# An FFN with all 22 column pairs in seven half-size products, two of the seven taken ahead for twelve pairs

## The chip, the cores and the metric

The kernel runs on one core of one Trainium2 chip. TensorE (PE in the profile) multiplies, VectorE (DVE) and ScalarE (ACT) prepare its operands and read its results, SyncE (SP) issues the loads. The metric is the device time of one execution in microseconds; the median of three runs is shown.

## The reference

One layer of a streaming-encoder block on 512 tokens of 1024 features, all in float32:

```python
def swiglu(x, w_gate, w_up, w_down):
    return (jax.nn.silu(x @ w_gate) * (x @ w_up)) @ w_down

h = h + 0.5 * rms_norm(swiglu(rms_norm(h, g1), gate1, up1, down1), g2)   # FFN1
h = h + rms_norm(hybrid_mixer(rms_norm(h, g3), ...), g4)                 # attention and convolution
h = h + 0.5 * rms_norm(swiglu(rms_norm(h, g5), gate2, up2, down2), g6)   # FFN2
```

Gate and up weights are 1024 x 2816, down weights 2816 x 1024. The change touches the first half of the two FFNs: silu(x @ w_gate) * (x @ w_up).

## The kernel before, in words

Every float32 operand is split into a high part (a cast to fp32r, on ACT) and a low part (the operand less its high part, on DVE); `split` issues the two. A product is then three matmuls per 128 x 128 weight tile (`mm3`: high x high, high x low, low x high). So each weight block of 128 x 1024 costs a load of 512 KB into one of three `raw` buffers, a cast on ACT (`whi<-raw`) and a subtraction on DVE (`wlo<-raw,whi`); the two parts lie in a ring of six.

The 2816 hidden features are 22 pairs; pair j is one block of gate weights and one of up weights, 128 features each. Before the change three pairs (`CLASSIC = 3`) are multiplied plainly: 2 blocks x 8 tiles x 3 matmuls over all 512 tokens. `hidden` then takes silu of the gate and multiplies it by up into the buffer `hid`. The other 19 pairs go through `seven_products`, which splits tokens and features in halves and makes the four quarter results of gate and up from seven products instead of eight: 7 x 4 tiles x 3 matmuls of 256 tokens, 84 in all. For this it needs sums of tokens (s1 to s4, `token_sums`, once per FFN: DVE sums, each split on ACT and DVE) and sums of weights for every pair: `t13` (up low half less gate low half, up high less up low) and `t24`. Split operands of a pair are `b` (the gate block itself), `t13`, `t24` and `b22` (the up block's second half).

`periods` runs one period per pair. In the period of pair j, TensorE takes the first three products of j (`b` x a11, `t13` x s1, `t24` x s2), the third products of the pair before, p (`t24` x a22, `b22` x s4), and the second products of j (`b` x a12, `t13` x s3). Meanwhile DVE and ACT prepare the next pair, n, and read the sums of j and p from PSUM. PE, DVE and ACT run in the order in which the code is written (`in_order`), each its own queue. At the start of an FFN the token quarters arrive late (`turn` transposes normed rows and splits them), so the plain pairs run first, on tokens 0 to 255 and then on the rest; the token sums and the first pair's operands (`before`, a generator stepped by `next`) are made beside them. After the 22 pairs comes the product with the down weights (`row_product`, L214), then the mixer, then FFN2 in the same way.

Of the kernel before, what the change touches and what calls it, by code (L numbers as in the profile page):

```python
# [14 lines left out]
P = 128  # L15
S = 512
# [28 lines left out]
CLASSIC = 3  # L45
# [7 lines left out]
def kernel(  # L53
# [41 lines left out]
    blocks = [w[i] for w in (w1, wm, w2) for i in range(w.shape[0])]  # L95
# [75 lines left out]
    def turn(t, xn, u):  # L171

        ts = slice(t * P, (t + 1) * P)
        pss = two_banks()
        for k in range(KD):
            nc.tensor.transpose(pss[k // 4][:, (k % 4) * P:(k % 4 + 1) * P], xn[:, k * P:(k + 1) * P], ident)  # L176
        for b, ps in enumerate(pss):
            ks = slice(4 * b, 4 * b + 4)
            split(u[0][:, ks, ts], u[1][:, ks, ts], ps.rearrange("p (k c) -> p k c", c=P))
# [112 lines left out]
    def token_sums(u, hid, gu):  # L292


        def scratch(i):
            return hid[:, 6 + 2 * i:8 + 2 * i, :].rearrange("p a (b c) -> p (a b) c", c=HALF)

        whole = {q: scratch(4 + i) for i, q in enumerate(((0, 0), (0, 1), (1, 0), (1, 1)))}
        s1, s2, s3, s4 = [scratch(i) for i in range(4)]
        parts = [[gu.tile([P, 4, HALF], F32R, name=f"s{i}{p}") for p in "hl"] for i in (1, 2, 4)]  # L300
        third = [gpool.tile([P, 4, HALF], F32R, name="gain") for _ in range(2)]

        def join(kb, tb):
            q = quadrant(u, kb, tb)
            nc.vector.tensor_tensor(out=whole[kb, tb], in0=q[0].bitcast(F32), in1=q[1].bitcast(F32), op=ALU.add)

        def early():
            join(0, 0)
            join(1, 0)


        def first():
            join(0, 1)
            join(1, 1)
            nc.vector.tensor_tensor(out=s1, in0=whole[0, 1], in1=whole[1, 1], op=ALU.add)
            nc.vector.tensor_tensor(out=s2, in0=s1, in1=whole[0, 0], op=ALU.subtract)
            split(*parts[0], s1)
            split(*parts[1], s2)

        def second():  # L320
            nc.vector.tensor_tensor(out=s4, in0=whole[1, 0], in1=s2, op=ALU.subtract)
            nc.vector.tensor_tensor(out=s3, in0=whole[0, 0], in1=whole[0, 1], op=ALU.subtract)
            split(*parts[2], s4)
            split(*third, s3)

        return parts[0], parts[1], third, parts[2], (early, first, second)

    def seven_products(u, sums, hid, gu, j0, acts):
# [4 lines left out]
        s1, s2, s3, s4, _ = sums  # L333
# [4 lines left out]
        def load(j):  # L338
            if j < NF:
                fetch(2)  # L340
                raw[j] = coming.pop(0), coming.pop(0)
# [20 lines left out]
        def parts(j, n):  # L362
            high(j, n)
            low(j, n)
# [9 lines left out]
        def product(ps, j, n, half, a, start=False):  # L374
            w = ops[j][n][0]
            for k in range(4):
                c0 = half * 512 + k * P

                mm3(ps[:, 0:HALF], part(w, ALLP, slice(c0, c0 + P)), part(a, ALLP, k), start and k == 0, k == 3,
                    skip_group_check=not start)  # L380

        def first_products(j):
            g[j] = [bank() for _ in range(3)]
            product(g[j][0], j, "b", 0, a11, start=True)
            product(g[j][2], j, "t13", 0, s1, start=True)
            product(g[j][1], j, "t24", 0, s2, start=True)

        def second_products(j):
            p7 = g[j][1], j, "t13", 1, s3
            p2 = g[j][0], j, "b", 1, a12  # L390

            for p in (p7, p2) if j == NF - 1 else (p2, p7):
                product(*p)

        def third_products(j):
            product(g[j][1], j, "t24", 1, a22)
            product(g[j][2], j, "b22", 0, s4)

        def silu(out, src):
            nc.scalar.activation(out=out, in_=src, func=AF.Silu)  # L400

        def before():

            load(j0)
            sums13(j0)
            parts(j0, "b")
            parts(j0, "t13")
            sums24(j0)
            yield
            parts(j0, "t24")  # L410
            yield
            parts(j0, "b22")
            load(j0 + 1)
# [8 lines left out]
        def first_sum(j):  # L422
            xs[j] = wide()
            nc.scalar.copy(out=xs[j][:, q[0]], in_=g[j][0][:, q[0]])

        def second_sum(j):
            add(xs[j][:, q[1]], g[j][1][:, q[0]], xs[j][:, q[0]])

        def periods():
            for j in range(j0, NF + 1):  # L430
                p, n = j - 1, j + 1
                old, now, new = p >= j0, j < NF, n < NF
                if old:
                    x, (g1, g2, g3) = xs[p], g[p]
                    y = ys[p] = wide()
                    add(x[:, q[2]], g2[:, q[0]], x[:, q[0]])
                    add(y[:, q[3]], g3[:, q[0]], x[:, q[2]])
                    silu(y[:, q[0]], g1[:, q[0]])
                if now:
                    first_products(j)  # L440
                if new:
                    sums13(n)
                    parts(n, "b")
                elif now:
                    prefetch(1)
                if now:
                    first_sum(j)

                if j == j0:
                    second_sum(j)  # L450
                    sums24(n)
                    parts(n, "t13")
                elif new:
                    parts(n, "t13")
                    second_sum(j)
                    sums24(n)
                elif now:
                    prefetch(2)
                    second_sum(j)
                if old:  # L460
                    third_products(p)
                    add(x[:, q[3]], g2[:, q[0]], x[:, q[0]])
# [10 lines left out]
                load(j + 2)  # L473
# [3 lines left out]
        return before(), periods  # L477

    def ffn(u, steps, post, late, pre=None, turned=None, between=None, weave=False):


        with tc.tile_pool(name="ffn_h", bufs=1) as hp:
            hid = hp.tile([P, NF, S], F32, name="hid")

            def hidden(j, ps):
                sh = wide()
                later["silu"] = nc.scalar.activation(out=sh[:, 0:S], in_=ps[0], func=AF.Silu)
                nc.vector.tensor_tensor(out=hid[:, j, :], in0=sh[:, 0:S], in1=ps[1], op=ALU.mult)

            with tc.tile_pool(name="ffn_gu", bufs=1) as gu:  # L490
                acts = []
                sums = token_sums(u, hid, gu)
                early, first, second = sums[-1]
                before, periods = seven_products(u, sums, hid, gu, CLASSIC, acts)
                ws = []
                head = len(steps)
                pss = [two_banks() for _ in range(head // 2)]
                with in_order():
                    for lo in (0, HALF):
                        for i in range(head):  # L500
                            if lo == 0:
                                for step in steps[i]:
                                    (step or early)()
                                ws.append(weight(0))
                            if lo == 0 and weave and i < 2:
                                for j, n in ((), ((0, 0), (0, 1), (1, 0), (0, 2), (1, 1), (1, 2)))[i]:
                                    one_part(ws[j], u, pss[0][j], 0, HALF, n)
                                continue
                            columns(ws[i], u, pss[i // 2][i % 2], lo, lo + HALF, by_part=lo == 0)
                        if lo == 0:  # L510
                            prefetch(2 * CLASSIC - head)
                            first()
                    hidden(0, pss[0])
                    next(before)
                    hidden(1, pss[1])
# [3 lines left out]
                with in_order():  # L519
                    next(before)  # L520
                    second()
                    for j in range(2, CLASSIC):
                        if j >= len(pss):
                            pss.append(two_banks())
                            for ps in pss[j]:
                                columns(weight(0), u, ps)
                        hidden(j, pss[j])
                    next(before, None)
# [13 lines left out]
    xns = {}  # L542

# [17 lines left out]
    def turned0(t):  # L561
        turn(t, xns[t][0], u1)
# [65 lines left out]
    with tc.tile_pool(name="mix", bufs=1) as mix:  # L628
# [240 lines left out]
        with tc.tile_pool(name="mixb", bufs=1) as mb:  # L869
# [60 lines left out]
            def turned2(t):  # L930
                if not u2:
                    u2.append(new_u())
                turn(t, xns[t], u2[0])
# [99 lines left out]
```

## Time and profile before

| | |
|---|---|
| median of three runs | 1038.58 us (1038.31 to 1040.38) |
| the profiled execution | 1038.58 us, of which the span is 1036.5 us |
| TensorE busy in the span | 1028.9 us (99%) |
| VectorE busy | 773.0 us (75%) |
| ScalarE busy | 476.0 us (46%) |
| loads of 512 KB, issue to landing | 3.6 us |

The profile is of the run that is also the median; some 2 us lie around the span. In the timeline views a row begins with its start in us from the span's start and its length; in square brackets stands the idle time of the engine ahead of it and who ended it.

### The profile page before, as it was taken

Reading aid. Unit: us, or ns where it says so; the run is one execution under the profiler, and the core shown is the slowest. Engines: PE = TensorE matmul, PEld = TensorE weight load, DVE = VectorE, ACT = ScalarE, POOL = GpSimd, SP = SyncE. Lnnn points to the kernel's source line nnn. Section 1 sums busy time; section 2 is a strip of 40 time slices with the busy share of each in tenths; the row PEclk is TensorE's granted clock in tenths of the full one; section 3 lists DMA queues with packets and bytes.
Section 4 is the critical chain, followed back from the end, with each engine's and each line's share of the span. In section 5 each row is a group of like instructions: output and inputs, shape, how many; then the busy total and the mean of one; then the engine's idle time right before and its main releaser. Section 6 shows DMA issues by size and latency. Waiting matters only on the chain.

```text
span 1036.5 us, 16089 instructions
## 1 busy us (share of the span) xinstructions
PE 1028.9 (99%) x6527; PEld 936.1 (90%) x6527; DVE 773.0 (75%) x1188; ACT 476.0 (46%) x785; POOL 20.3 (2%) x42
## 2 busy tenths in 40 slices
PE   9999999999999999999999999999999999999997
PEld 8999999998888898888888888899999999988886
DVE  7999989896332659999869776489989898963314
ACT  6444444444321532677874444354444444442311
POOL 1000000000000100000000100010000000000000
PEclk9999999999999999999999999999999999999999
DMA  6233333336333033433222145131433333353202
GB/s 244 67 103 101 113 98 117 102 114 197 97 102 102 26 119 99 128 95 99 87 77 62 41 131 172 44 102 42 116 98 113 102 102 103 126 181 91 92 21 82
DMA packets 30044, 106.40 MB, mean 103 GB/s; under 512 B 3457, under 2 KB 4105, under 8 KB 29970
## 3 DMA queue, kind: packets, MB, share of 16 engines
q1 hardware_dynamic: 27648, 100.41, 31.0%
q10 hardware_dynamic: 2322, 4.97, 1.5%
q8 instruction: 51, 0.84, 0.3%
q14 instruction: 23, 0.19, 0.1%
HBM read 103.25 MB, written 2.12 MB: 102 GB/s over the span
## 4 chain that ended last, share of the span: by engine, by line
PE 97%; DVE 2%; ACT 1%; issue 0%; DVEq 0%; POOLq 0%; POOL 0%; ACTq 0%
PE ps L214 27%; PE ps L131 20%; PE ps L133 20%; PE ps L132 20%; PE ps L196 5%; PE ps L176 1%; PE ps L832 1%; PE ps L815 1%; DVE acc L643 1%; PE ps L805 0%; PE ps L804 0%; PE ps L275 0%; DVE ptl L93 0%; PE ps L569 0%; DVE wlo L93 0%
## 5 line engine op out<-in xcount | busy, mean ns | idle before, releaser
L131 PE MATMUL ps<-uh,whi 128*128 128x256 f32 (+1 forms) x808 | 254.7, 315 | 0.0
L133 PE MATMUL ps<-uh,wlo 128*128 128x256 f32 (+1 forms) x808 | 252.7, 313 | 0.0
L132 PE MATMUL ps<-ul,whi 128*128 128x256 f32 (+1 forms) x808 | 252.6, 313 | 0.0
L93 DVE TENSOR_TENSOR wlo<-raw,whi 128x1024 fp32r<-128x1024 f32 x108 | 131.5, 1221 | 132.5 <-ACT whi L92 130.7
L92 ACT CAST whi<-raw 128x1024 fp32r<-128x1024 f32 x108 | 112.8, 1051 | 164.6 <-PE ps L214 126.9
L214 PE MATMUL ps<-whi,act 128*128 128x512 f32 x640 | 172.7, 389 | 0.0
L133 PEld LDWEIGHTS ps<-uh,wlo 128*128 128x128 f32 x808 | 154.2, 191 | 9.0
L132 PEld LDWEIGHTS ps<-ul,whi 128*128 128x128 f32 x808 | 154.3, 191 | 8.0
L131 PEld LDWEIGHTS ps<-uh,whi 128*128 128x128 f32 x808 | 154.2, 191 | 8.0
L368 ACT CAST whi<-t 128x1024 fp32r<-128x1024 f32 x76 | 79.8, 1051 | 174.6 <-DVE t L344 165.6
L214 PEld LDWEIGHTS ps<-whi,act 128*128 128x128 f32 x640 | 120.0, 188 | 24.8
L372 DVE TENSOR_TENSOR wlo<-t,whi 128x1024 fp32r<-128x1024 f32 x76 | 93.1, 1226 | 29.1 <-ACT whi L368 29.0
L214 PE MATMUL ps<-wlo,act 128*128 128x512 f32 x320 | 99.3, 389 | 0.0
L643 DVE SCALAR_TENSOR_TENSOR acc<-c,ch,acc 128x512 f32<-128x512 f32 x120 | 86.2, 746 | 1.5
L344 DVE TENSOR_TENSOR xn<-ps,xn 128x256 f32<-128x256 f32 x190 | 79.5, 419 | 5.0 <-PE ps L133 3.6
L214 PEld LDWEIGHTS ps<-wlo,act 128*128 128x128 f32 x320 | 60.1, 188 | 12.5
L344 DVE TENSOR_TENSOR t<-raw,t 128x512 f32<-128x512 f32 x76 | 52.2, 687 | 1.3
L344 DVE TENSOR_TENSOR t<-raw 128x512 f32<-128x512 f32 x76 | 48.8, 684 | 0.0
L372 DVE TENSOR_TENSOR wlo<-raw,whi 128x1024 fp32r<-128x1024 f32 x38 | 46.3, 1219 | 0.0
L131 PE MATMUL ps<-gain,whi 128*128 128x256 f32 x152 | 43.2, 284 | 0.0
L131 PE MATMUL ps<-s1h,whi 128*128 128x256 f32 x152 | 43.0, 283 | 0.0
L132 PE MATMUL ps<-s1l,whi 128*128 128x256 f32 x152 | 43.0, 283 | 0.0
(203 smaller groups left out, 1903.3 us busy)
## 6 DMA issues: line engine op xcount, KB each, us to landing
raw<-in_w SPq DMA_DIRECT2D x132, 512.0 KB, 3.6
raw<-in_wm SPq DMA_DIRECT2D x52, 512.0 KB, 3.6
gain<-in_gains ACTq DMA_DIRECT2D x5, 512.0 KB, 4.0
h<-in_x SPq DMA_DIRECT2D x4, 512.0 KB, 7.6
out<-h SPq DMA_DIRECT2D x3, 512.0 KB, 2.6
bias<-tab_d ACTq DMA_DIRECT2D x8, 128.0 KB, 3.1
bias<-tab_d ACTq DMA_DIRECT2D x8, 112.0 KB, 2.9
out<-xn SPq DMA_DIRECT2D x1, 256.0 KB
```

Source lines behind the costliest of these rows:

```text
L92: nc.scalar.copy(out=hi, in_=src)
L93: nc.vector.tensor_tensor(out=lo, in0=src, in1=hi.bitcast(F32), op=ALU.subtract)
L131: nc.tensor.matmul(ps, a[0], b[0], start=start, stop=False, **kw)
L132: nc.tensor.matmul(ps, a[0], b[1], start=False, stop=False, **kw)
L133: nc.tensor.matmul(ps, a[1], b[0], start=False, stop=stop, **kw)
L176: nc.tensor.transpose(pss[k // 4][:, (k % 4) * P:(k % 4 + 1) * P], xn[:, k * P:(k + 1) * P], ident)
L196: nc.tensor.matmul(ps[:, lo:hi], w[wi][:, k * P:(k + 1) * P], u[ui][:, k, lo:hi], start=i == 0 and k == 0, stop=i == 2 and k == KD - 1)
L214: nc.tensor.matmul(acc[n], a[ai], w[bi][:, n * 512:(n + 1) * 512], start=start and i == 0, stop=stop and i == 2)
L344: nc.vector.tensor_tensor(out=out, in0=a, in1=b, op=op)
L368: nc.scalar.copy(out=h_, in_=src)
L372: nc.vector.tensor_tensor(out=l_, in0=src, in1=h_.bitcast(F32), op=ALU.subtract)
L643: nc.vector.scalar_tensor_tensor(acc[:, j, :], cs[j][:, w:w + S], wc, acc[:, j, :], op0=ALU.mult, op1=ALU.add)
```

## The change

All 22 pairs go through `seven_products`; `CLASSIC` and `hidden` are gone. For the pairs 0 to 11 (`EARLY = 12`) the two products of `b` are taken ahead: `early_products` multiplies the gate block by tokens 0 to 255, keeps the first product (`hid[:, j, 0:HALF]`) and silu of the sum of both (`hid[:, j, HALF:]`). These twelve stand where the plain pairs stood. When such a pair comes up in `periods`, it has no `b`: five products, 60 matmuls; the other ten pairs keep seven. `ORDER` mixes the two kinds. The gate blocks of the twelve are loaded twice, once for `early_products` and once as part of their pair.

The token sums and the first pair's operands are made in eight steps (`first` and `before`, four each) between the early products; the last two sums (`second`) follow in the first period. `turn` writes the unsplit tokens (`whole`) by a second ACT copy from PSUM where before DVE added the two parts.

```diff
-CLASSIC = 3
+EARLY = 12
+ORDER = [12, 0, 13, 1, 14, 2, 15, 3, 4, 16, 5, 17, 6, 7, 18, 8, 19, 9, 10, 20, 11, 21]
@@ turn @@
             split(u[0][:, ks, ts], u[1][:, ks, ts], src)
+            if whole:
+                nc.scalar.copy(out=whole[b, 1][:, :, t % 2 * P:(t % 2 + 1) * P], in_=src)
@@ token_sums: first and second @@
+            nc.vector.tensor_tensor(out=s12, in0=whole[0, 1], in1=whole[1, 1], op=ALU.add)
+            high(s1, s12)
+            yield
+            low(s1, s12)
+            yield
+            nc.vector.tensor_tensor(out=s12, in0=s12, in1=whole[0, 0], op=ALU.subtract)
+            high(s2, s12)
+            yield
+            low(s2, s12)
+            yield
...
@@ seven_products @@
-            ops[j] = {"b": (pair_tiles(), gate), "t13": (pair_tiles(), t13)}
+            ops[j] = {"t13": (pair_tiles(), t13)}
+            if j >= EARLY:
+                ops[j]["b"] = pair_tiles(), gate
...
+        def early_products(j, w):
+            ps = bank()
+            product(ps, w, 0, a11, start=True)
+            nc.scalar.copy(out=hid[:, j, 0:HALF], in_=ps[:, 0:HALF])
+            product(ps, w, 1, a12)
+            later["silu"] = silu(hid[:, j, HALF:], ps[:, 0:HALF])
...
         def periods():
-            for j in range(j0, NF + 1):
+            for i in range(NF + 1):
+                p, j, n = [ORDER[x] if 0 <= x < NF else None for x in (i - 1, i, i + 1)]
...
-                    silu(y[:, q[0]], g1[:, q[0]])
+                    if g1:
+                        silu(y[:, q[0]], g1[:, q[0]])
+                    else:
+                        nc.scalar.copy(out=y[:, q[0]], in_=hid[:, p, HALF:])
                 if now:
                     first_products(j)
+                if i == 0:
+                    second()
                 if new:
                     sums13(n)
                     parts(n, "b")
...
@@ ffn @@
+                        if j >= head:
+                            prefetch(min(2, EARLY - j))
+                            for _ in range(8 * (j + 1 - head) // (EARLY - head) - 8 * (j - head) // (EARLY - head)):
+                                next(todo.pop(0))
...
+                        early_products(j, weight(0))
```

Two places in the order of the instructions. The first is VectorE's queue in a steady period of FFN1. Before, with the next pair's `t13` as t_729 and `t24` as t_743:

```order
L344 TENSOR_TENSOR xn<-ps,xn 128x256 x2
L344 TENSOR_TENSOR t_729<-raw 128x512 x2
L372 TENSOR_TENSOR wlo<-raw,whi 128x1024
L372 TENSOR_TENSOR wlo<-t_729,whi 128x1024
L344 TENSOR_TENSOR xn<-ps,xn 128x256
L344 TENSOR_TENSOR t_743<-raw,t_729 128x512
L344 TENSOR_TENSOR t_743<-raw,t_743 128x512
L344 TENSOR_TENSOR xn<-ps,xn 128x256
L372 TENSOR_TENSOR wlo<-t_743,whi 128x1024
L344 TENSOR_TENSOR xn<-ps,xn 128x256
L470 TENSOR_TENSOR hid<-xn 128x512
L372 TENSOR_TENSOR b22l<-raw,b22h 128x512
```

VectorE's queue in the change, in the period in which pair 1, one of the twelve, is the next (`t13` is t_934, `t24` t_944):

```order
L366 TENSOR_TENSOR xn<-ps,hid 128x256
L366 TENSOR_TENSOR xn<-ps,xn 128x256
L366 TENSOR_TENSOR t_934<-raw 128x512 x2
L397 TENSOR_TENSOR wlo<-t_934,whi 128x1024
L366 TENSOR_TENSOR xn<-ps,xn 128x256
L366 TENSOR_TENSOR t_944<-raw,t_934 128x512
L366 TENSOR_TENSOR t_944<-raw,t_944 128x512
L366 TENSOR_TENSOR xn<-ps,hid 128x256
L397 TENSOR_TENSOR wlo<-t_944,whi 128x1024
L366 TENSOR_TENSOR xn<-ps,xn 128x256
L528 TENSOR_TENSOR hid<-xn 128x512
L397 TENSOR_TENSOR b22l<-raw,b22h 128x512
```

The row `wlo<-raw,whi`, the low part of `b`, is gone from between the sums of `t13` and the low part of `t13`; all else stands where it stood. For a next pair that is not one of the twelve the queue is as before.

The second is ScalarE's queue in FFN1 in the change, between the early products of the gates 5 and 9 (a `CAST whi<-raw` is the high part of a coming gate block, an `ACTIVATE hid<-ps` the silu of a finished early product, which TensorE must have ended):

```order
L452 ACTIVATE hid<-ps 128x256
L94 CAST whi<-raw 128x1024
L316 CAST s2h<-hid 128x1024
L652 DMA tab_d<-xn 8x640
L430 COPY hid<-ps 128x256
L452 ACTIVATE hid<-ps 128x256
L94 CAST whi<-raw 128x1024
L430 COPY hid<-ps 128x256
L452 ACTIVATE hid<-ps 128x256
L94 CAST whi<-raw 128x1024
L393 CAST whi<-t_553 128x1024
```

These silus are of the gates 5, 6 and 7, and the casts behind them those of the gates 7, 8 and 9: a gate's cast stands behind the silu of the gate two before it. Before, no cast of a weight block of the plain pairs stood behind a silu.

## Rows read from the trace of the kernel before

**Rows 1.** The page: the span, and each engine's busy time, share and instructions.

```profile
span 1036.5 us, 16089 instructions
PE 1028.9 (99%) x6527; PEld 936.1 (90%) x6527; DVE 773.0 (75%) x1188; ACT 476.0 (46%) x785; POOL 20.3 (2%) x42
```

**Rows 2.** Stretches of FFN1 (start and periods): length, busy per engine, granted clock, DMA.

```profile
10.00:58.50 48.50, 48.50 (x356) 46.39 (x355) 45.95 (x57) 24.92 (x35) 2.03 (x4) 0.98 0.37 119
58.50:230.00 171.50, 171.50 (x1431) 171.50 (x1431) 154.36 (x237) 77.70 (x120) 0.00 (x0) 1.00 0.34 104
```

**Rows 3.** Timeline of TensorE: plain pair, one product in two periods, start of down products.

```profile
46.36 0.39 PE L131 MATMUL ps<-uh,whi 128*128 128x512 f32 x1
46.59 0.39 PE L132 MATMUL ps<-ul,whi 128*128 128x512 f32 x1
...
103.19 0.28 PE L131 MATMUL ps<-gain,whi 128*128 128x256 f32 x1
...
113.27 0.28 PE L131 MATMUL ps<-gain,whi 128*128 128x256 f32 x1
...
238.55 0.63 PE L214 MATMUL ps<-whi 128*128 128x512 f32 x2
...
910.50 0.63 PE L214 MATMUL ps<-whi 128*128 128x512 f32 x2
```

**Rows 4.** Timeline of VectorE in one period of FFN1.

```profile
106.89 0.88 DVE L344 TENSOR_TENSOR xn<-ps,xn 128x256 f32<-128x256 f32 x2
107.68 1.28 DVE L344 TENSOR_TENSOR t<-raw 128x512 f32<-128x512 f32 x2
108.88 1.22 DVE L372 TENSOR_TENSOR wlo<-raw,whi 128x1024 fp32r<-128x1024 f32 x1
110.08 1.23 DVE L372 TENSOR_TENSOR wlo<-t,whi 128x1024 fp32r<-128x1024 f32 x1
...
111.56 1.41 DVE L344 TENSOR_TENSOR t<-raw,t 128x512 f32<-128x512 f32 x2
...
114.14 1.23 DVE L372 TENSOR_TENSOR wlo<-t,whi 128x1024 fp32r<-128x1024 f32 x1 [0.83 <-ACT whi L368]
...
117.01 0.88 DVE L344 TENSOR_TENSOR xn<-ps,xn 128x256 f32<-128x256 f32 x2
```

**Rows 5.** Timeline of ScalarE in the same period.

```profile
103.89 0.41 ACT L400 ACTIVATE xn<-xn 128x256 f32<-128x256 f32 x1
...
106.91 0.38 ACT L424 COPY xn<-ps 128x256 f32<-128x256 f32 x1
109.00 1.05 ACT L368 CAST whi<-t 128x1024 fp32r<-128x1024 f32 x1 [1.72 <-DVE t L344]
```

**Rows 6.** Timeline of VectorE: first and last of FFN1's 17 steady `hid` products.

```profile
65.17 0.69 DVE L470 TENSOR_TENSOR hid<-xn 128x512 f32<-128x512 f32 x1
...
227.22 0.69 DVE L470 TENSOR_TENSOR hid<-xn 128x512 f32<-128x512 f32 x1
```

**Rows 7.** Timeline of VectorE: last token split, first period's low parts, FFN1 and FFN2.

```profile
22.13 1.29 DVE L93 TENSOR_TENSOR ul<-ps,uh 128x512 fp32r<-128x512 f32 x2
...
53.29 2.42 DVE L372 TENSOR_TENSOR wlo<-t,whi 128x1024 fp32r<-128x1024 f32 x2
...
698.69 1.29 DVE L93 TENSOR_TENSOR ul<-ps,uh 128x512 fp32r<-128x512 f32 x2 [0.35 <-ACT uh L92]
...
725.56 2.42 DVE L372 TENSOR_TENSOR wlo<-t,whi 128x1024 fp32r<-128x1024 f32 x2
```

**Rows 8.** The load queue's waits in FFN1's periods (total, times, longest); landing times.

```profile
SPq L103 <- DVE t L344: 96.0, 17, 5.7
...
DMA to landing us min/median/max: 3.4/3.5/4.4
```

**Rows 9.** Stretches of 1 us at the start (columns as in rows 2).

```profile
9.00:10.00 1.00, 1.00 (x6) 1.00 (x6) 1.00 (x2) 0.69 (x3) 0.00 (x0) 0.50 1.01 414
...
13.00:14.00 1.00, 1.00 (x11) 1.00 (x9) 1.00 (x1) 1.00 (x3) 0.52 (x1) 1.00 0.53 213
```

More of the change, by code (lines that the diff above doesn't have):

```diff
@@ L292, in token_sums @@
     def token_sums(u, hid, gu):
[L295 to L305, printed above, removed]
+        whole = {}
@@ new lines, in token_sums, with high, low @@
+        for i, x in enumerate(((0, 0), (0, 1), (1, 0), (1, 1))):
+            at = hid[:, 14 + 2 * i:16 + 2 * i, :]
+            whole[x] = at.rearrange("p a (b c) -> p (a b) c", c=HALF)
+        s12 = whole[1, 1]
+        s1, s2, s4 = [[gu.tile([P, 4, HALF], F32R, name=f"s{i}{p}") for p in "hl"] for i in (1, 2, 4)]
+        s3 = [gpool.tile([P, 4, HALF], F32R, name="gain") for _ in range(2)]
+        def high(s, src):
+            nc.scalar.copy(out=s[0], in_=src)
+        def low(s, src):
+            nc.vector.tensor_tensor(out=s[1], in0=src, in1=s[0].bitcast(F32), op=ALU.subtract)
@@ L332, in seven_products @@
+        return s1, s2, s3, s4, whole, (early, first(), second)
+    def seven_products(u, sums, hid, gu, acts):
         a11, a12, a22 = quadrant(u, 0, 0), quadrant(u, 1, 0), quadrant(u, 1, 1)
-        s1, s2, s3, s4, _ = sums
+        s1, s2, s3, s4, _, (_, _, second) = sums
         raw, ops, g, xs, ys = {}, {}, {}, {}, {}
@@ L382, in first_products @@
         def first_products(j):
[L383 to L386, printed above, removed]
-        def second_products(j):
[L389 to L393, printed above, removed]
-        def third_products(j):
-            product(g[j][1], j, "t24", 1, a22)
-            product(g[j][2], j, "b22", 0, s4)
+            g[j] = [j >= EARLY and bank(), bank(), bank()]
@@ new lines, in third_products, with woven_products, taken @@
+        def third_products(j):
+            product(g[j][1], ops[j]["t24"][0], 1, a22)
+            product(g[j][2], ops[j]["b22"][0], 0, s4)
+        def early_products(j, w):
[4 more added lines that the diff above has]
+            later["silu"] = silu(hid[:, j, HALF:], ps[:, 0:HALF])
+        def woven_products(ws):
+            pss = [two_banks() for _ in ws]
+            for j, i in ((0, 0), (0, 1), (1, 0), (0, 2), (1, 1), (1, 2)):
+                wi, ui = ((0, 0), (1, 0), (0, 1))[i]
+                for k in range(KD):
+                    nc.tensor.matmul(pss[j][k // 4][:, 0:HALF], ws[j][wi][:, k * P:(k + 1) * P], u[ui][:, k, 0:HALF],
+                                     start=i == 0 and k % 4 == 0, stop=i == 2 and k % 4 == 3)
+            def taken():
+                for j, (p1, p2) in enumerate(pss):
+                    nc.scalar.copy(out=hid[:, j, 0:HALF], in_=p1[:, 0:HALF])
+                    add(hid[:, j, HALF:], p2[:, 0:HALF], hid[:, j, 0:HALF])
+                    silu(hid[:, j, HALF:], hid[:, j, HALF:])
+            return taken
@@ L399, in silu @@
         def silu(out, src):
-            nc.scalar.activation(out=out, in_=src, func=AF.Silu)
+            return nc.scalar.activation(out=out, in_=src, func=AF.Silu)
         def before():
[L404 to L408, printed above, removed]
+            j = ORDER[0]
+            load(0)
+            sums13(j)
+            high(j, "t13")
             yield
-            parts(j0, "t24")
+            low(j, "t13")
             yield
-            parts(j0, "b22")
@@ L413, in before @@
-            load(j0 + 1)
+            sums24(j)
+            high(j, "t24")
+            yield
+            low(j, "t24")
+            parts(j, "b")
+            yield
         def down_parts(n):
@@ L492, in ffn @@
                 sums = token_sums(u, hid, gu)
-                early, first, second = sums[-1]
-                before, periods = seven_products(u, sums, hid, gu, CLASSIC, acts)
-                ws = []
+                early, first, _ = sums[-1]
+                early_products, woven_products, before, periods = seven_products(u, sums, hid, gu, acts)
+                todo = [x for x in (first,) * 4 + (before,) * 4]
                 head = len(steps)
-                pss = [two_banks() for _ in range(head // 2)]
@@ L516, in ffn @@
+                wholes.append(sums[4])
+                woven = []
+                with in_order():
+                    early_pairs(range(head + 1))
                 if between:
@@ L519, in ffn @@
                 with in_order():
[L520 to L528, printed above, removed]
+                    early_pairs(range(head + 1, EARLY))
                     periods()
```

140 lines of the change are left out of this document (71 added, 69 removed).

## Prediction

> **What bounds the kernel now.** I read the page first: TensorE is busy through 99% of the span and VectorE through 75% [rows 1]. By that TensorE is the bound, and fewer matmuls are less time. The table of stretches narrows this: in the periods of FFN1 TensorE is full, at the full granted clock, and VectorE is busy for 154.36 of 171.50 us, 90% [rows 2]. The change adds work for VectorE in just this stage, so the question is how much room the missing 10% is.
>
> The timelines answer it. On TensorE the same product returns after 113.27 - 103.19 = 10.08 us [rows 3]; a period has 84 matmuls, so one of 256 tokens takes 0.120 us. On VectorE the `hid` product returns (227.22 - 65.17) / 16 = 10.13 us later [rows 6]: VectorE's cycle is slightly **longer** than TensorE's, and it falls back by 0.05 us in each period. In its own row of work [rows 4] it hardly waits for TensorE: its one wait of size is 0.83 us, for ScalarE, ahead of the low part of `t24`. So VectorE already runs at its own pace, and 10.13 us is a chain: DVE makes a sum, ACT casts it to the high part, DVE subtracts for the low part, twice in each period (`t13`, `t24`), with DVE's other work between. TensorE stays full only because VectorE started a little ahead. That lead is small: in the period shown the low part of `t24` (of pair 10) is ready at 114.14 + 1.23 = 115.37 us [rows 4], so that of pair 5 at 64.7 and that of pair 21, 11 cycles on, at 226.8; from there TensorE needs 84 more matmuls, 10.1 us; the down products start at 238.55 us [rows 3]: 1.7 us of lead are left.
>
> **The change part by part.** *Matmuls.* Removed in FFN1: two plain pairs in halves (192 matmuls x 0.120) and one pair of 48 wide ones at 46.59 - 46.36 = 0.23 us [rows 3], 33.9 us; in FFN2 three pairs in halves, 288 x 0.120 = 34.6 us. Added in each: three pairs x 84 x 0.120 = 30.2 us. TensorE saves 3.7 + 4.3 = 8.0 us. The moved products (24 per early gate, 2.88 us) cost the same in either place.
>
> *A period whose next pair is one of the twelve.* TensorE's own five products take 60 x 0.120 = 7.2 us instead of 10.08. What does VectorE's cycle lose? Only the low part of `b`, 1.20 us from 108.88 to 110.08 [rows 4]. But ScalarE casts `t13` from 109.00 to 110.05 [rows 5], and the low part of `t13` starts at 110.08 [rows 4]. The low part of `b` did nothing but fill that wait. Taken out, it leaves VectorE idle for those 1.2 us, since its queue has the low part of `t13` next and runs in order. The price of the cycle stays 10.13 us; the bounds are 10.13 (the cast decides) and 8.93 (the whole 1.20 us is saved, if something else hid the cast). I take 10.13, because both rows end at the same 0.03 us. The 0.83 us wait for `t24` stays too: nothing around it moves.
>
> *Does something else come into the cycle?* A load could: the next pair's up block takes the buffer of this pair's gate block, free after the `t24` sums (111.56 + 1.41 = 112.97). SP waits for just that, up to 5.7 us, and a load lands in 3.5 us [rows 8], so at some 116.6; the next `t13` sums come at 107.68 + 10.13 = 117.8. Hidden, with about 1 us to spare, and the second loading of the gates is part of the same two loads per period. A cycle of 10.13 does not get slower by it. TensorE's sums are always there in time: after the low part of `t24` it needs 12 matmuls (1.4 us) to the sum that VectorE reads some 6 us later.
>
> *The steady stage.* Now all 22 pairs pass through this chain. Let R be the time at which `t24` of the second pair in the order is ready. From there: one shorter cycle (9.0 us, as before from 53.29 + 2.42 = 55.71 [rows 7] to 64.7), 19 cycles of 10.13, and TensorE's last 84 matmuls: 9.0 + 192.5 + 10.1 = 211.6 us to the down products. Before, the same way took 238.55 - 55.71 = 182.8 us in FFN1 and 910.50 - 727.98 = 182.5 us in FFN2 [rows 3, 7]. That is **28.8 + 29.1 = 57.9 us** more: three more cycles less the lead, in each FFN.
>
> *The start.* R is later as well. I followed VectorE's, ScalarE's and TensorE's queues from the last token split on, with 1.18 us for a DVE operation on 1024 (these start 1.20 us apart or a little less), 1.05 us for a cast, 0.4 us for a copy or silu of 256 [rows 4, 5], 2.88 us for a gate. Before, from the end of that split to R took 55.71 - 23.42 = 32.3 us in FFN1 and 727.98 - 699.98 = 28.0 us in FFN2 [rows 7]. Now the split ends later, by 4.0 and 1.9 us: ScalarE has four copies of `whole` and the copies and silus of the first gates ahead of it. Behind it stand 22 such operations and 6.6 us of smaller ones in FFN1 (32.6 us; FFN2 19 and 6.0, 28.4 us): about as much as before. But they wait: the cast of a gate stands behind the silu of the gate two before, which waits for TensorE to end that gate; with a token sum and its low part put between two gates' low parts on VectorE, that ring is slower than 2.88 us per gate. In FFN1 I find 1.4, 2.5 and 2.9 us for the gates 7, 8 and 10, 3.1 us for casts of sums and 0.9 us for `b` and `b22`, 10.9 us in all; in FFN2 11.2 us in the same way. So R is later by 4.0 + 0.3 + 10.9 = 15.2 us and by 1.9 + 0.4 + 11.2 = 13.5 us, **28.7 us** together. Bounds: without the waits for gates (6.8 us in FFN1, some 7 in FFN2) about 14 us together are left; with twice these waits it is 43 us.
>
> *What costs nothing.* The copies of `whole` in place of two DVE sums, silu of a short pair replaced by a copy: ScalarE is busy for 77.70 of 171.50 us [rows 2]; once VectorE were no longer the chain, a copy would cost its 0.4 us.
>
> **Sum**: 1038.58 + 57.9 + 28.7 = **1125 us**. The profiled execution is the median of the runs, so no correction; the 8.0 us of saved matmuls are spent as TensorE's waiting, since it now has 72 matmuls (8.64 us) in most cycles of 10.13.
>
> **A rule against this.** By busy time VectorE has (154.36 / 171.50) x 10.13 = 9.1 us a period with `b` and 7.9 without, 186 us for 22 pairs; TensorE has 10 x 10.08 + 12 x 7.2 = 187.2 us. The Trainium skill, page "Perfetto Trace Analysis", section "Identifying the Most-Contended Engine", says to find the limiting engine by occupancy, for VectorE too. By that rule TensorE stays the bound and the sum would be 1038.58 - 8.0 = 1030.6 us; by the row of the cycle, in which VectorE waits 0.83 us for ScalarE and still has no time to spare, it is 1125. This trace speaks against the rule: at 90% busy VectorE's cycle is already the longer one.
>
> **The rivals.** *TensorE stays the bound*: 1030.6 us. For it: the busy sums above. Against it: the chain is 10.13 us whatever is taken out of its covered wait. It decides for itself where the mean cycle is under TensorE's own 187.2 / 22 = 8.5 us; with R as late as I find it, no gain is left above 10.13 - 43.3 / 19 = 7.9 us. *Only work counts*: the cast of `t13` is hidden somehow and each of the 24 short preparations saves its 1.20 us: 1125 - 28.8 = 1096 us. Against it: there is nothing in the queue ahead of that low part. *The clock falls*: at the start the granted clock is at 1.2 GHz (0.50) from 9 to 12 us, behind a stretch of sparse matmuls, and back at 2.4 GHz in the 14th us [rows 9]. TensorE will now wait 1.5 us in most cycles and nearly 3 where two short pairs follow each other. At half the clock a cycle's 72 matmuls take 17.3 us instead of 8.64, 7.2 us over the cycle; if that befell one cycle in four of 40, 72 us more: about 1197 us. The Trainium skill, "TensorE: Matmul & The Clock Gate", section "HAM oscillation — how this bites in real kernels", warns of just such gaps between bursts; no stretch of this trace at steady work has one, so nothing here shows whether these are long enough. *Something between* (VectorE's chain, but an early stage without waits and a gain in the cycles): 1040 to 1094 us.
>
> **How the numbers follow.** The chain as worked out 0.72, its own range 1110 to 1139 us by the bounds of the start; only work 0.12; TensorE bound 0.07; the clock 0.05; something between 0.04. The range 1094 to 1142 takes in the first two, 84 in 100. Under 0.2%, some 2 us, a measurement can't tell a difference. Faster by more 0.07, within it 0.01, slower 0.92.
>
> **What would show it.** In the profile after: the `hid` product returns every 10.1 us for short and full pairs alike, with 1.1 us of VectorE's idle time for ScalarE ahead of the low part of `t13` of a short pair and 0.83 us ahead of `t24`; TensorE waits in every period for the low part of `t24`, some 1.5 us; the periods of an FFN last some 29 us longer, its start 13 to 15. I am wrong if short periods return in less than 9 us, if TensorE's idle time ends on a load, or if the granted clock falls in the periods.

## The result and the profile after

The changed kernel takes 1183.93 us (median of four runs, 1182.26 to 1186.05), against 1039.48 us for the kernel before beside it: a ratio of 1.139, 95% interval 1.138 to 1.141. The prediction of 1125 us had the direction and missed the size by 59 us; the time lies outside its range of 1094 to 1142 us.

The page of the kernel after, in the parts that answer to [rows 1]: span, busy time of each engine, the granted clock in 40 slices of 29.5 us, and the shares of the chain that ended last.

```profile
span 1180.4 us, 16203 instructions
PE 1066.3 (90%) x6503; PEld 954.0 (81%) x6503; DVE 808.3 (68%) x1252; ACT 505.5 (43%) x841; POOL 20.8 (2%) x42
PEclk9889999999999999999999999988999999999999
PE 55%; DVE 31%; ACT 10%; issue 3%; POOL 0%; DMA 0%; DVEq 0%; POOLq 0%; ACTq 0%
```

TensorE is idle for 1180.4 - 1066.3 = 114 us where it was idle for 8 [rows 1], and the clock line has a dent at the front of each FFN. Stretches of the kernel after, with the columns of [rows 2]: four of 10 us in FFN1's start, and the periods.

```profile
20.00:30.00 10.00, 3.98 (x24) 3.65 (x23) 4.27 (x7) 3.61 (x9) 0.00 (x0) 0.70 0.32 105
...
50.00:60.00 10.00, 6.90 (x35) 6.61 (x36) 3.87 (x5) 3.01 (x5) 0.00 (x0) 0.66 0.22 74
60.00:70.00 10.00, 6.13 (x39) 5.72 (x37) 2.61 (x4) 4.00 (x7) 0.00 (x0) 0.83 0.26 88
70.00:80.00 10.00, 3.40 (x25) 3.19 (x26) 5.25 (x6) 3.07 (x5) 0.00 (x0) 0.93 0.34 106
...
110.00:300.00 190.00, 166.82 (x1320) 160.13 (x1320) 159.71 (x255) 72.32 (x109) 0.00 (x0) 1.00 0.32 105
```

In the periods TensorE is at 88% and VectorE at 84%, both below what they were, at a granted clock of 1.00. In the four stretches of the start nobody is full: TensorE works 3.4 to 6.9 of 10 us, VectorE and ScalarE 2.6 to 5.3, where TensorE was full before [rows 2]. In the other stretches from 30 to 100 us TensorE works 6.4 to 9.5 of 10 us.

VectorE's timeline after, with the marks that divide it: the last token split of FFN1's start, the end of both starts (the low part of `t24` of the second pair, R in the prediction), two cycles of the periods, the first token split on the way to FFN2. The last row, by itself, is that split in the kernel before.

```profile
35.13 0.69 DVE L95 TENSOR_TENSOR ul<-ps,uh 128x512 fp32r<-128x512 f32 x1 [1.14 <-ACT uh L94]
...
99.76 1.23 DVE L397 TENSOR_TENSOR wlo<-t,whi 128x1024 fp32r<-128x1024 f32 x1 [1.17 <-ACT whi L393]
...
135.06 1.23 DVE L397 TENSOR_TENSOR wlo<-t,whi 128x1024 fp32r<-128x1024 f32 x1 [1.11 <-ACT whi L393]
...
139.06 1.22 DVE L397 TENSOR_TENSOR wlo<-t,whi 128x1024 fp32r<-128x1024 f32 x1 [0.78 <-ACT whi L393]
...
140.72 0.69 DVE L528 TENSOR_TENSOR hid<-xn 128x512 f32<-128x512 f32 x1
...
150.85 0.69 DVE L528 TENSOR_TENSOR hid<-xn 128x512 f32<-128x512 f32 x1
...
160.92 0.69 DVE L528 TENSOR_TENSOR hid<-xn 128x512 f32<-128x512 f32 x1
...
745.45 1.28 DVE L95 TENSOR_TENSOR ul<-ps,uh 128x512 fp32r<-128x512 f32 x2
...
841.21 1.23 DVE L397 TENSOR_TENSOR wlo<-t,whi 128x1024 fp32r<-128x1024 f32 x1 [1.17 <-ACT whi L393]
```

```profile
671.67 1.28 DVE L93 TENSOR_TENSOR ul<-ps,uh 128x512 fp32r<-128x512 f32 x2
```

These marks divide the loss. R comes at 100.99 us in place of 55.71 [rows 7]: 45.3 us in FFN1's start. The token split at 745.45 stood at 671.67 us before: 73.8 us for FFN1 in all, so 28.5 for its periods. In FFN2 R comes at 842.44 in place of 727.98 [rows 7], 114.5 later, 40.7 of it from this start; the spans differ by 143.9, which leaves 29.4 for FFN2's periods. The same division for the experiments that follow (us more than before, each from the same three marks and the span of its profiled run):

| | start FFN1 | periods FFN1 | start FFN2 | periods FFN2 | sum |
|---|---|---|---|---|---|
| forecast | 15.2 | 28.8 | 13.5 | 29.1 | 86.6 |
| after | 45.3 | 28.5 | 40.7 | 29.4 | 143.9 |
| e1, second product later | 26.7 | 28.5 | 25.2 | 29.5 | 109.9 |
| e2, sums of `t24` earlier | 41.7 | 5.0 | 38.5 | 5.6 | 90.9 |
| e3, both | 23.0 | 5.0 | 22.5 | 5.7 | 56.2 |
| e4, filler matmuls | 47.0 | 28.7 | 52.8 | 29.1 | 157.5 |
| e6, extra operation behind `t13` | 42.4 | 42.4 | 41.2 | 43.4 | 169.4 |
| e7, e3 with steps behind | 24.0 | 5.0 | 23.7 | 5.6 | 58.4 |
| e8, e7 with gate blocks ahead | 18.8 | 5.0 | 20.5 | 5.7 | 49.9 |
| e10, e8 without copies of `whole` | 17.4 | 5.0 | 21.8 | 6.2 | 50.3 |

Some 2.2 us of the 45.3 are not the change's. FFN1's first token split begins at 22.05 us in this execution and at 19.74 before; but in e6, whose code is the same up to there, it begins at 19.87. In the executions shown of e3, e6 and e9 it begins as early as before, so e3's 23.0 and e6's 42.4 stand for some 2 us more beside the other rows.

So the steady stage cost what was forecast, 57.9 us, and the starts 86.0 where 28.7 was forecast. What the stages wait for, in the table of waits (engine and line, released by; total, times, longest): first FFN1's start from 10 to 100 us, then the periods from 100 to 280.

```profile
DVE wlo L95 <- ACT whi L94: 28.2, 8, 5.7
...
PE ps L139 <- ACT hid L430: 25.7, 9, 6.2
ACT hid L452 <- PE ps L141: 22.3, 10, 3.0
```

```profile
DVE wlo L397 <- ACT whi L393: 25.9, 28, 1.2
...
PE ps L139 <- DVE xn L366: 19.2, 21, 1.2
...
PE ps L141 <- DVE wlo L397: 3.6, 11, 0.8
```

In the start, the three engines wait for each other for about the same time, in a circle. L430 is the copy of the first early product out of its PSUM bank. One turn of the circle is seen in the timelines of ScalarE, TensorE and VectorE around 65 us:

```profile
64.14 1.04 ACT L393 CAST whi<-t 128x1024 fp32r<-128x1024 f32 x1 [2.50 <-DVE t L366]
65.09 0.37 ACT L430 COPY hid<-ps 128x256 f32<-128x256 f32 x1
68.47 0.39 ACT L452 ACTIVATE hid<-ps 128x256 f32<-128x256 f32 x1 [3.02 <-PE ps L141]
68.75 1.04 ACT L94 CAST whi<-raw 128x1024 fp32r<-128x1024 f32 x1
```

```profile
61.44 0.28 PE L141 MATMUL ps<-uh,wlo 128*128 128x256 f32 x1
65.51 0.58 PE L139 MATMUL ps<-uh,whi 128*128 128x256 f32 x1 [3.79 <-ACT hid L430]
65.89 0.41 PE L140 MATMUL ps<-ul,whi 128*128 128x256 f32 x1
66.10 0.41 PE L141 MATMUL ps<-uh,wlo 128*128 128x256 f32 x1
...
68.23 0.37 PE L139 MATMUL ps<-uh,whi 128*128 128x256 f32 x1
...
69.52 0.28 PE L140 MATMUL ps<-ul,whi 128*128 128x256 f32 x1
69.64 0.28 PE L141 MATMUL ps<-uh,wlo 128*128 128x256 f32 x1
```

```profile
62.82 1.29 DVE L366 TENSOR_TENSOR t<-raw 128x512 f32<-128x512 f32 x2
69.82 1.23 DVE L95 TENSOR_TENSOR wlo<-raw,whi 128x1024 fp32r<-128x1024 f32 x1 [5.72 <-ACT whi L94]
```

VectorE's sums for `t13` end at 64.1; only then can ScalarE cast them, and only behind that cast does its queue come to the copy. TensorE ended the first product at 61.7 (61.44 + 0.28), but the second product adds into the same bank that the copy must first read. It starts at 65.51, and up to 68.23 at the lower level of the clock, 1.2 GHz (0.21 us from one matmul to the next at 65.89 and 66.10, against 0.12 at 69.52 and 69.64); the table of stretches shows a granted clock of 0.50 there:

```profile
65.51:68.23 2.72, 2.72 (x12) 2.72 (x13) 0.00 (x0) 0.00 (x0) 0.00 (x0) 0.50 0.10 41
```

The silu waits 3.02 us for this product, the next gate's cast stands behind the silu, and VectorE waits 5.72 us for that cast.

My first theory (A) was therefore: the start is a ring of waits that passes through the copy between the two products, and the periods are the chain of the prediction. The rivals: the fallen clock (C) makes the start long; the work itself, in its order on ScalarE and VectorE, makes it long (B), whatever TensorE does.

### The profile page after: what moved, and what is told of

Its sections match the earlier page's. It is cut to its first block, busy times and chain, and to the rows that moved or that the text cites. A ratio compares the mean times of both kernels' runs of the same rounds, so it can differ in the third digit from the quotient of the medians.

```text
span 1180.4 us, 16203 instructions
## 1 busy us (share of the span) xinstructions
PE 1066.3 (90%) x6503; PEld 954.0 (81%) x6503; DVE 808.3 (68%) x1252; ACT 505.5 (43%) x841; POOL 20.8 (2%) x42
## 3 DMA queue, kind: packets, MB, share of 16 engines
q1 hardware_dynamic: 31104, 113.00, 29.4%
## 4 chain that ended last, share of the span: by engine, by line
PE 55%; DVE 31%; ACT 10%; issue 3%; POOL 0%; DMA 0%; DVEq 0%; POOLq 0%; ACTq 0%
PE ps L225 23%; DVE wlo L397 10%; DVE t L366 9%; PE ps L139 9%; PE ps L141 9%; PE ps L140 9%; ACT whi L393 6%; DVE xn L366 4%; DVE hid L528 2%; DVE b22l L397 2%; PE ps L207 1%; DVE wlo L95 1%; ACT whi L94 1%; PE ps L881 1%; PE ps L864 1%
## 5 line engine op out<-in xcount | busy, mean ns | idle before, releaser
L139 PE MATMUL ps<-uh,whi 128*128 128x256 f32 (+1 forms) x768 | 255.5, 333 | 67.5 <-ACT hid L430 49.7
L95 DVE TENSOR_TENSOR wlo<-raw,whi 128x1024 fp32r<-128x1024 f32 x120 | 146.2, 1222 | 178.1 <-ACT whi L94 176.7
L139 PEld LDWEIGHTS ps<-uh,whi 128*128 128x128 f32 x768 | 153.7, 200 | 85.0 <-ACT hid L430 54.2
L94 ACT CAST whi<-raw 128x1024 fp32r<-128x1024 f32 x120 | 124.8, 1049 | 165.6 <-PE ps L225 128.1
L393 ACT CAST whi<-t 128x1024 fp32r<-128x1024 f32 x88 | 92.2, 1048 | 225.2 <-DVE t L366 221.9
L397 DVE TENSOR_TENSOR wlo<-t,whi 128x1024 fp32r<-128x1024 f32 x88 | 107.8, 1225 | 63.4 <-ACT whi L393 63.3
L139 PE MATMUL ps<-gain,whi 128*128 128x256 f32 x176 | 52.7, 300 | 29.1 <-DVE xn L366 29.1
L366 DVE TENSOR_TENSOR xn<-ps,xn 128x256 f32<-128x256 f32 x148 | 62.2, 420 | 3.0 <-PE ps L141 1.5
L366 DVE TENSOR_TENSOR t<-raw,t 128x512 f32<-128x512 f32 x88 | 60.4, 687 | 1.5
L139 PEld LDWEIGHTS ps<-gain,whi 128*128 128x128 f32 x176 | 33.3, 189 | 34.2 <-DVE xn L366 34.2
L141 PE MATMUL ps<-s2h,wlo 128*128 128x256 f32 x176 | 52.3, 297 | 7.6 <-DVE wlo L397 7.5
L366 DVE TENSOR_TENSOR t<-raw 128x512 f32<-128x512 f32 x88 | 56.5, 683 | 0.0
L139 PE MATMUL ps<-s2h,whi 128*128 128x256 f32 x176 | 50.0, 284 | 2.0 <-ACT whi L393 2.0
```

Of the source, the lines that this page charges most:

```text
L94: nc.scalar.copy(out=hi, in_=src)
L95: nc.vector.tensor_tensor(out=lo, in0=src, in1=hi.bitcast(F32), op=ALU.subtract)
L139: nc.tensor.matmul(ps, a[0], b[0], start=start, stop=False, **kw)
L141: nc.tensor.matmul(ps, a[1], b[0], start=False, stop=stop, **kw)
L366: nc.vector.tensor_tensor(out=out, in0=a, in1=b, op=op)
L393: nc.scalar.copy(out=h_, in_=src)
```

## Experiments

**e1: the second product of a gate behind the first of the next.** TensorE gets another product to do while the copy comes.

```diff
             nc.scalar.copy(out=hid[:, j, 0:HALF], in_=ps[:, 0:HALF])
-            product(ps, w, 1, a12)
-            later["silu"] = silu(hid[:, j, HALF:], ps[:, 0:HALF])
+            late_product()
+            waiting.append((j, w, ps))
+            if j == EARLY - 1:
+                late_product()
...
+        def late_product():
...
+            if waiting:
+                j, w, ps = waiting.pop()
+                product(ps, w, 1, a12)
+                later["silu"] = silu(hid[:, j, HALF:], ps[:, 0:HALF])
```

> The second early product of a gate is put behind the first one of the next gate on TensorE; no engine gets more or less work. Theory A (the start of an FFN is long because TensorE waits, between the two products of a gate, for ScalarE's copy out of the same bank): the two starts lose most of the 58 us that my forecast missed, 1184 becomes about 1127 us (1115 to 1145), and the rows of TensorE waiting for the copy of hid are gone. Rival B (the start is set by ScalarE's casts that stand behind silus and by VectorE's token sums, or by the fallen clock alone): under 20 us gained, above 1164 us.

Measured: 1147.99 us, 1.105 (1.103 to 1.106) of before; 36 us less than the changed kernel. Its waits from 10 to 100 us:

```profile
DVE wlo L95 <- ACT whi L94: 12.7, 6, 3.6
...
PE ps L139 <- ACT hid L430: 7.6, 6, 2.1
```

TensorE's wait for the copy fell by 18.1 us, and FFN1's start by 18.6; the periods did not move. With FFN2's 15.5 us, the order of these two products gives back 34.1 of the 57.3 us by which the starts exceed the forecast: the larger part of the miss is shown. But I had expected 57 us, 1115 to 1145, not 36: the ring is weaker, not gone.

**e2: the sums of `t24` directly behind those of `t13`** on VectorE in the periods, so that it has work while ScalarE casts `t13`.

```diff
                     sums13(n)
+                    sums24(n)
                     parts(n, "b")
...
                         parts(n, "t13")
-                    sums24(n)
```

> In each period the two sums of t24 are made directly behind those of t13, so that each cast of a sum has other VectorE work beside it; amount of work unchanged. Theory A (the cycle of 10.1 us is a chain of sum, cast, low part, twice): the two waits for casts go, cycles become some 8.1 us short and 9.2 us full where TensorE allows it, mean about 8.7 us since TensorE needs 8.5; 40 cycles gain about 56 us: 1128 us (1118 to 1140), the starts unchanged. Rival B (the cycle is set by the amount of VectorE's work, by loads, or by the queue of ScalarE): within 10 us of 1184.

Measured: 1129.49 us, 1.087 (1.085 to 1.089) of before, 54.4 us less. By the table 47 of them are from the periods; nearly 6 are from the starts, which I had expected unchanged (R lies in a first period with the same chain). The same operations in another order: the chain was the price. Loads were not: in the changed kernel's periods no engine's wait from 100 to 280 us ends on a load.

**e3: both.**

> Both edits. Theory A: the gains are in different stages and add: 1184 - 57 - 56 = 1071 us (1058 to 1088), still above 1039 because the first steady period begins later than before. Rival B (one bound behind both): not below 1110 us.

Measured: 1095.94 us, 1.055 (1.052 to 1.057) of before. 88 us less, where the two alone gave 36 + 54: independent, as two stages in a row should be; that it is not the 1058 to 1088 I had expected is e1's miss again. VectorE's timeline in a period for a short pair:

```profile
122.93 0.69 DVE L539 TENSOR_TENSOR hid<-xn 128x512 f32<-128x512 f32 x1
...
124.93 1.28 DVE L366 TENSOR_TENSOR t<-raw 128x512 f32<-128x512 f32 x2
126.13 1.41 DVE L366 TENSOR_TENSOR t<-raw,t 128x512 f32<-128x512 f32 x2
127.47 1.22 DVE L397 TENSOR_TENSOR wlo<-t,whi 128x1024 fp32r<-128x1024 f32 x1
...
129.27 1.22 DVE L397 TENSOR_TENSOR wlo<-t,whi 128x1024 fp32r<-128x1024 f32 x1
...
130.92 0.69 DVE L539 TENSOR_TENSOR hid<-xn 128x512 f32<-128x512 f32 x1
```

Both waits for a cast (1.11 and 0.78 us in the kernel after) are gone. The `hid` products of FFN1 now return after 8.0 us (122.93 to 130.92) and 9.9 in turn where a short and a full pair alternate, after 8.8 and 9.1 where two short ones stand together: 8.8 on average, close to TensorE's own mean of 8.5.

**e4: 24 more matmuls into a spare bank between the two early products,** results unused, to keep TensorE running while the copy comes.

```diff
             nc.scalar.copy(out=hid[:, j, 0:HALF], in_=ps[:, 0:HALF])
+            spare = bank()
+            for i in range(2):
+                product(spare, w, 0, a11, start=True)
             product(ps, w, 1, a12)
```

> 24 more matmuls, into a spare bank whose result nobody reads, between the two early products of each gate from the third on in FFN1 and of all in FFN2: 2.9 us of work at the full clock, put where TensorE waits. Theory A (the wait for ScalarE's copy sets the start, the fallen clock is its consequence and costs 1.5 us in about five gates of an FFN): TensorE's clock stays near 1.00 in the starts, time saved in the long waits is spent in the short ones, 1170 to 1200 us. Rival C (the fallen clock is the main cause of the long starts): under 1150 us.

Measured: 1195.95 us, 1.150 (1.147 to 1.153) of before, 12 us more than the changed kernel. Its stretches in FFN1's start:

```profile
50.00:60.00 10.00, 9.16 (x77) 8.96 (x76) 3.38 (x3) 4.33 (x7) 0.00 (x0) 1.00 0.20 56
60.00:70.00 10.00, 9.09 (x76) 8.89 (x76) 3.77 (x5) 2.64 (x4) 0.00 (x0) 1.00 0.36 105
```

The clock stood at 1.00 where it had been 0.66 and 0.83, and FFN1's start was 47.0 us late in place of 45.3, FFN2's 52.8 in place of 40.7. This alone does not settle what the clock costs: the filler adds 24 x 0.12 = 2.9 us of matmuls to every gate, which can eat what the clock gives. But the changed kernel's trace bounds it. In its two starts 94 and 82 matmuls of 256 columns stand 0.21 us before the next in place of 0.12, so these can have cost at most 176 x 0.093, some 16 us, of the 86.0: rival C is not the main cause. In e1 there are 45 and 46 such matmuls, so up to 8 of its 34 us may be the clock's.

**e5 and e6: one VectorE operation too many per short period,** a sum of 1024 columns (1.2 us; its result is not used). In e5 it stands where the low part of `b` was taken out, in e6 behind the low part of `t13`.

```diff
+                if new and n < EARLY and i:
+                    junk(n)              # e5: behind the sums of t13
                 if now:
...
                         parts(n, "t13")
+                    if n < EARLY and i:
+                        junk(n)          # e6: here instead
                     sums24(n)
```

> The changed kernel with one more VectorE operation (a sum of 1024 columns that nobody uses) in each of the 22 steady periods whose next pair is one of the twelve, between the t13 sums and the low part of t13: just where the low part of b stood. Theory A (that place is idle time that the cast of t13 covers): short cycles 10.06 become 10.13 us at most, 1184 becomes 1184 to 1187 us. Rival B (VectorE's amount of work counts): 22 x 1.2 = 26 us more, 1210 us.

> The same extra operation in the same 22 periods, but behind the low part of t13 and ahead of the t24 sums, where nothing covers it. Theory A: each of the 22 cycles becomes 1.15 to 1.2 us longer, 1184 + 26 = 1210 us (1206 to 1212). Rival C (the steady cycle has room, something else sets it): within 5 us of 1184.

Measured, one run each: 1182.39 us for e5, the changed kernel's own time, and 1207.92 for e6, 25.5 more. VectorE in a short period of e5 (the third operation of the first row is the extra one), then of e6 (the extra one is at 135.01):

```profile
132.58 2.42 DVE L366 TENSOR_TENSOR t<-raw 128x512 f32<-128x512 f32 x3
134.97 1.23 DVE L402 TENSOR_TENSOR wlo<-t,whi 128x1024 fp32r<-128x1024 f32 x1
```

```profile
131.14 1.28 DVE L366 TENSOR_TENSOR t<-raw 128x512 f32<-128x512 f32 x2
133.54 1.23 DVE L402 TENSOR_TENSOR wlo<-t,whi 128x1024 fp32r<-128x1024 f32 x1 [1.11 <-ACT whi L398]
...
135.01 1.22 DVE L366 TENSOR_TENSOR t<-raw 128x1024 f32<-128x1024 f32 x1
```

The same 1.2 us is free while the cast runs (the wait of 1.11 us is gone in e5, and short cycles stay at 10.07 us) and costs its full length behind it: short cycles of 11.32 us, 1.26 more, 22 times, some 28 us; the table has 13.9 more in the periods of either FFN. The difference of the two times is smaller, 25.5, because in e6's execution FFN1 began 2.2 us earlier. This is the step "the low part of `b` did nothing but fill that wait", tested by itself.

**e7: e3 with the eight preparation steps issued behind the early product of a gate** instead of ahead of it.

```diff
-                            for _ in range(8 * (j + 1 - head) // (EARLY - head) - 8 * (j - head) // (EARLY - head)):
-                                next(todo.pop(0))
...
                         early_products(j, weight(0))
+                        if j >= head:
+                            for _ in range(8 * (j + 1 - head) // (EARLY - head) - 8 * (j - head) // (EARLY - head)):
+                                next(todo.pop(0))
```

> Both edits of e3, and the eight steps that make the token sums and the first pair's operands are issued behind a gate's early product instead of ahead of it, so that ScalarE's copy no longer queues behind the cast of a token sum. Theory A (what is left of the long start is ScalarE's queue order: the copies and the casts of the coming gates wait behind casts that wait for VectorE): 15 to 30 us less than e3's 1096, 1066 to 1081 us. Rival B (the rest is the amount of work on VectorE and ScalarE in the start): within 6 us of 1096.

Measured: 1095.95 us, 1.054 (1.052 to 1.056): e3's time. What I expected of it, 15 to 30 us, was wrong: the place of the steps within a gate does not change the time.

**e8: e7 with the gate blocks loaded, cast and split further ahead.**

```diff
-                            prefetch(min(2, EARLY - j))
+                            prefetch(min(4, EARLY - j))
```

(and the list of blocks, which sets the order of the loads, begins with 12 gates in place of 10 and 11).

> As e7, and the gate blocks are cast and split up to four ahead instead of two (the order of the loads follows). Theory A (the ring silu of a gate, cast of the gate two on, low part, product sets the pace where a token sum lies between): 8 to 20 us less than e7, 1050 to 1070 us. Rival B (depth does not matter, the amount of work does): within 4 us of e7.

Measured: 1088.17 us, 1.047 (1.045 to 1.049), 7.8 us less than e7, just short of the 8 to 20 expected. ScalarE waits for a load once, 2.8 us (4.7 in two waits in e7), and the casts come closer: VectorE's wait for `whi` at L95 is 4.6 us from 10 to 100 us, against 10.7 in e7. A late load was a link in the changed kernel too: ahead of the cast at 74.66 us ScalarE waited 2.15 us for one, and the longest of TensorE's waits for the copy, 6.2 us, ends at 79.74.

**e9: the kernel before with e2's order.** Was the chain already the bound there?

```diff
                     sums13(n)
+                    sums24(n)
                     parts(n, "b")
...
                     second_sum(j)
-                    sums24(n)
                     parts(n, "t13")
```

> The kernel before, with the t24 sums directly behind the t13 sums in each period, as in e2. Theory A (before the change TensorE is the bound and VectorE's chain of 10.13 us just fits under it): VectorE's cycle gets its 0.83 us of waiting back and keeps to TensorE's 10.08 us, but the time does not move: within 2 us of before (about 1039.5). Rival B (VectorE's chain already cost time before): 2 us or more faster, the 1.7 us of lead per FFN turning into less waiting at the joints.

Measured: 1039.48 us beside 1038.43, a ratio of 1.001 (1.000 to 1.002). No gain, although VectorE's `hid` product now returned every 10.08 us in place of 10.13: before, TensorE was the bound, and VectorE's chain, slower by 0.05 us a period, was covered by its lead.

**e10: e8 with the copies of `whole` on ScalarE undone,** two VectorE sums per FFN instead, as before the change.

> As e8, but the unsplit tokens 256 to 511 are made by two VectorE sums per FFN as before the change, and ScalarE's four copies out of the transposes' banks are gone. Theory A (these copies wait for VectorE's reading of the same bank and hold up ScalarE, and TensorE waits for them for the next banks, some 2 us in FFN1): 2 to 8 us less than e8's 1088. Rival B (the 2.4 us more of VectorE work per FFN in the start weigh as much): within 2 us of e8.

Measured: 1088.48 us, 1.047 (1.046 to 1.049): e8's time, not the 2 to 8 us less of theory A. The token split ended earlier (28.9 in place of 32.4 us), but R only by 1.4 us in FFN1, and FFN2's start is 1.3 us longer, by the table: what the copies delay is waited for again behind them.

## Why the prediction was right and wrong

**The steady stage: right, to 0.1 us in the sum** (28.5 + 29.4 against 28.8 + 29.1; each half is off by 0.3, and that these cancel is luck). The cycle is 10.13 us where the next pair is full (140.72 to 150.85) and 10.07 where it is short, against a forecast of 10.13 for both; the two waits stand where they were put, 1.11 and 0.78 us. e5, e6 and e2 show the mechanism: covered work is free, uncovered work costs all of its length, and a different order alone takes 47 us back. One detail was wrong: TensorE was to wait for the low part of `t24`, 1.5 us in most cycles. Those waits are 3.6 us in all from 100 to 280 us; 19.2 end on VectorE's reading of sums (`PE ps L139 <- DVE xn L366`). The larger ones, of up to 1.2 us, stand ahead of `t13` x s3 of a short pair, first VectorE's reading, then TensorE's product:

```profile
126.09 0.42 DVE L366 TENSOR_TENSOR xn<-ps,hid 128x256 f32<-128x256 f32 x1
```

```profile
126.56 0.39 PE L139 MATMUL ps<-gain,whi 128*128 128x256 f32 x1 [1.21 <-DVE xn L366]
```

This product adds into the bank in which `t24` x s2 stands, VectorE must read the bank between the two, and that reading stands behind the low part of `t13`. So the periods have in small what the starts have in large: a reader's queue between two products of one bank.

**The rule of occupancy.** In the periods no engine is full, with TensorE at 88% and VectorE at 84%, and yet the cycle has no room. So this trace speaks against the rule of the Trainium skill ("Perfetto Trace Analysis", "Identifying the Most-Contended Engine") for this kernel: no engine got less work in e2, and the periods became 47 us shorter. Of the kernel before the prediction said so too soon. There occupancy named the right engine, TensorE at 99%: VectorE's cycle was the longer one by 0.05 us, but e9 took that away and gained nothing.

**The start: wrong, 86.0 us where the sum had 28.7.** The step that failed is "The moved products (24 per early gate, 2.88 us) cost the same in either place", and with it the ring of waits behind it, which I worked out from 2.88 us for a gate. The two products of a gate write one bank, and the copy between them is ScalarE's, whose queue stands behind silus, casts of sums and casts of the next gate. So TensorE does not take 2.88 us for a gate but waits up to 6.2 us in the middle of it, 25.7 us in FFN1. I had followed the three queues, but only the waits at the start and the end of a gate. Both parts of that term came out too small. The last token split ended 12.4 us later in FFN1 (35.82; 4.0 forecast, and some 2.2 lie ahead of FFN1) and 18.7 in FFN2 (792.48, less the 73.8 of FFN1, against 699.98 [rows 7]; 1.9 forecast); from there to R it took 32.9 us more in FFN1 (11.2 forecast) and 22.0 in FFN2 (11.6 forecast). The copy is in the first part too: the transposes ahead of the split stand in TensorE's queue behind a second product that waits for it.

```profile
27.84 0.58 PE L139 MATMUL ps<-uh,whi 128*128 128x256 f32 x1 [5.76 <-ACT hid L430]
...
30.57 1.19 PE L184 MATMUL ps<-ident,xn 128*128 128x128 f32 x8
```

e1 takes 18.6 and 15.5 us of the two starts back by moving the second product alone; 3.4 and 9.6 of them are the split's.

**What is left is open.** In e8 the starts are 18.8 and 20.5 us late, 39.3 together, still more than the 28.7 of the sum. The token split's end is 9.0 and 9.5 us late (32.44 us, of which some 2.2 lie ahead of FFN1, and 733.31 in FFN2 less the 23.8 of FFN1), the way from there to R 10 to 11 us longer. e7 and e10 show that neither the place of the steps nor the copies of `whole` are the cause; gate blocks taken further ahead were worth 8 us. Which link of the remaining ring is the longest was not settled.

**The rivals.** TensorE does not stay the bound, and short periods save nothing. The price of "the clock falls", 1197 us, is near the measured time, but not by its mechanism: it put the fall in the periods, where 1.00 was granted throughout. The clock fell in the starts, behind waits of 3.8 to 6.2 us; e4, which lifted it there, did not shorten the starts, and the slower matmuls can have cost some 16 us at most. The starts agree with the warning of the Trainium skill ("TensorE: Matmul & The Clock Gate", "HAM oscillation — how this bites in real kernels"), though the waits there are for loads and here for another engine's copy; the periods, with waits of up to 1.2 us, show no fall. The bound of 43 us on the starts was too low because it doubled the waits that I had found, and the missed wait was not among them.

## What to carry to other kernels

Where two products add into one bank and another engine must read the bank between them, that reader's whole queue stands in the middle of the matmuls: issue another product between the two, as e1 did, and cost the moved work by its slowest reader, not by its matmuls. Before work is taken from a full-looking engine, look at what ended its idle time: here, what stood under another engine's cast could be taken out or put in for nothing, and an order that covers the cast (54 us in e2) was worth more than all the matmuls saved (8 us by the prediction's count). Even so no version of the change beat the kernel before: the best was 1.047 of it.

## What had not been expected of the hardware

TensorE's clock stayed at 1.00 (2.4 GHz) through 190 us of periods with waits of up to 1.2 us, while the four stretches of FFN1's start shown, with single waits of up to 6.2 us, were granted 0.66 to 0.93 on average: behind the wait of 3.79 us that ends at 65.51, TensorE ran its first 2.7 us at the lower of its two levels, 1.2 GHz.
